# The norms of the latent vectors: squares, sums and roots made within the input projections, not beside the first neighbourhood heads

## The chip, the cores and the metric

The kernel runs on one core of a Trainium2 chip. The engines have the profile's short names: PE is TensorE (matrix products; PEld its weight loads), DVE is VectorE, ACT is ScalarE, POOL is GpSimd and SP is SyncE, which here only issues DMA transfers. The metric is the device time of one execution in microseconds (us), and the median of several executions is the time of a kernel. A profiled execution gives the trace from which the rows below are taken; its span is the time from its first to its last instruction.

## The reference

Two consecutive layers of a diffusion backbone work on 512 latent tokens and 256 context tokens of 1024 features. Layer 0 has two groups of heads that share one input projection: eight latent-attention heads and eight neighbourhood heads. The part that the change touches is the norm of the low-rank vectors of the latent-attention heads. For each token the projection gives 256 features for the queries (`cq`) and 128 for keys and values (`ckv`); each of the two is divided by the root of its mean square and multiplied by a gain before it is projected up:

```python
def rms_norm(x, gain=None):
    y = x * rsqrt(mean(x * x, axis=-1) + EPS)
    return y * gain

q    = rms_norm(p[..., :256], q_norm) @ w_q_up       # 8 heads of 64 + 32
c_kv = rms_norm(p[..., 256:384], kv_norm)            # keys and values of 8 heads
k_rope = p[..., 384:416]                             # 32 rotated features
```

The neighbourhood heads (64 features each) attend in a two-dimensional grid of the latent tokens, with a bias that masks what lies outside a neighbourhood, and to the context. After the heads come the output projection and a gated feed-forward layer. Layer 1 has 16 windowed heads in place of both groups, again with a feed-forward layer, and a last norm ends the program.

## The kernel before

All tensors are held with features on the 128 partitions and the 768 tokens (512 latent, 256 context) along the free dimension. A product in 32-bit precision is made of three products of halves: a high part and a low part of each operand, of which the two low parts' product is left out. Lines L324, L325 and L326 are these three products of the projections; L311 and L312 make the two halves of a weight, and L348 and L349 (`split`) those of an activation.

The projections of layer 0 are one generator, `projections`. It first makes the query and key pairs of neighbourhood heads 0 to 3, and then goes through the string `AFTER = "012k5678"`: "0", "1" and "2" are the three latent tiles `lat_raw[0..2]` of 128 features and 768 tokens (0 and 1 are `cq`, 2 is `ckv`), "k" is the rotated key, and "5" to "8" are raw queries and keys of heads 4 to 7. Between its steps, side work is taken in: the rows of the modulation (`mod_tile`, lines L241 to L262), which multiply weights by the conditioning vector `cond`, on DVE by L241, or on POOL by L258 and on ACT by L259. `cond` goes through Silu first (L163). At the end of the projections a part of the modulation is made by PE instead, from weights that arrive as `ph` and `pl` (L191).

Then `attend(na_jobs())` runs the neighbourhood heads. For each block of queries PE makes scores (L749, L750), DVE adds the bias and finds the maximum in one instruction (L546, `take`), ACT takes the exponential (L542, `exps`), PE turns the result (L483, `turned`), DVE or ACT copies it out of PSUM (L474, L475), and PE multiplies it with the values (L536, `weighted`). L458 to L466 (`finish_pair`) divide by the sums. The bias tiles come from memory into a pool of two buffers named `nb`, 384 KB each, so that a new one can be loaded only when an older one has been read. Beside the heads, side work advances step by step, a step ending at each `yield`: the norms of the latent vectors (`latent_norms`, which calls `gained`) come first, then what prepares the latent heads.

`gained` has the squares on POOL (L921, since `SQ = 1`), the sum of the two `cq` squares on DVE (L925), the sum over partitions on PE by products with a column of ones (L928), Sqrt on ACT (L931), the reciprocal on DVE (L932), a spread of the 12 columns over partitions (`spread`, L453, on PE, and a copy on ACT, L940), the gains on DVE (L943) and the split into halves (L348, L349). Sqrt, Exp and Silu are held in different tables of ACT, so a change from one to another shows as `ACT_TABLE_LOAD`.

The order of the instructions on each engine isn't written out by hand. A list scheduler, with a simulated timeline, orders the recorded program by readiness and priority; instructions of the side work have a priority lowered by `LOWER = 150`. Buffers come from pools by name (`b` 24, `p` 8, `ph` and `pl` 4 each, `nb` 2, and so on), and PSUM banks of general use come from a ring of seven entries, `"stsdtsd"`, whose letters are the tags `pss`, `pst` and `psd` in the trace. All loads with plain `dma` are issued by SP in one queue (L134).

Of the kernel before, what the change touches and what calls it, by code (L numbers as in the profile page):

```python
# [15 lines left out]
P = 128  # L16
# [84 lines left out]
def hybrid_kernel(ctx: ExitStack, tc, I, out):  # L101
# [230 lines left out]
    def PQ():  # L332
        return PS("d")
# [576 lines left out]

    def gained(groups):

        d, m = PQ(), NT // P
        n = m * len(groups)
        col = T("sm", [P, 6, 2]).rearrange("p a b -> p (a b)")[:, :n]
        for i, (tiles, _) in enumerate(groups):
            acc = None
            for t in tiles:
                s = B()
                if SQ:  # L920
                    G.tensor_tensor(s, t, t, op=ALU.mult)  # L921
                else:
                    S.activation(s, t, AF.Square)
                if acc is not None:
                    V.tensor_tensor(s, s, acc, op=ALU.add)  # L925
                acc = s
            for j in range(m):
                PE.matmul(d[:, i * m + j : i * m + j + 1], acc[:, j * P : (j + 1) * P], ones[:, :1], start=True, stop=True)  # L928
        for i, (tiles, _) in enumerate(groups):
            c = slice(i * m, i * m + m)  # L930
            S.activation(col[:, c], d[:, c], AF.Sqrt, bias=eps, scale=1.0 / (P * len(tiles)))  # L931
        V.reciprocal(col, col)  # L932
        yield
# [20 lines left out]
    def projections():  # L954

        for p in range(2):
            yield from project_shifted(I["w_in0"][p], put_q(sets[p][0]), scale=0.125)
            yield from project_shifted(I["w_in0"][p + 4], put_k(sets[p][1], KC[0]))
        for x in AFTER:
            if x in "012":  # L960
                lat_raw[int(x)] = B()
                yield from project_shifted(I["w_in0"][8 + int(x)], put(lat_raw[int(x)]))
            elif x == "k":
                kr.append(B())
                yield from project_shifted(I["w_kr"], put_rope(kr[0], rope0, SWAP8, 32, tag="p"), m=32)
            else:
                raws.append(B(tag="p"))
                i = int(x) - 5
                yield from project_shifted(I["w_in0"][(2, 6, 3, 7)[i]], put(raws[i]), scale=(0.125, None)[i % 2])

# [30 lines left out]
    def latent_norms():  # L1001
        groups = [(lat_raw[2:], 2), (lat_raw[:2], 0)]
# [906 lines left out]
```

## Time and profile before

| what | value |
|---|---|
| three executions | 1591.6, 1584.18 and 1589.64 us, median 1589.64 |
| the profiled execution: its time, its span | 1587.21 us, 1585.4 us |
| mean granted clock of PE | 0.995 |
| busy share of the span: PE, PEld, DVE, ACT, POOL | 97%, 87%, 75%, 51%, 17% |
| transfers over the whole span | 214.95 MB, mean 136 GB/s |
| the projections' end and the first neighbourhood heads | about 198 us of the span |
| start of the first roots of the latent norms (L931) | 220.79 us |

A row of a timeline gives the start, the duration, the engine, the line, the operation, output and inputs by their names, shapes, and how often it stands in a row; in brackets stands the idle time of the engine ahead of it and what ended that. A row of waits says what an engine waited for, with the total, the number and the longest. A row of the chain gives the start, the duration and the kind of work that set the end at that time.

### The profile page before, as it was taken

The numbers are of one execution on the slowest core, as the hardware profiler recorded it, in microseconds if no ns is written. First come the engines' busy times: TensorE is split into PE (matmuls) and PEld (weight loads), VectorE is DVE, ScalarE is ACT, GpSimd is POOL, SyncE is SP. The second block draws the span as 40 slices with busy tenths as digits, with TensorE's granted clock in tenths as the row PEclk, the third lists the DMA queues.
The fourth block names the chain that finished last, engine by engine and source line by source line (L and its number), as shares of the span: only waits on it lengthen the run. The fifth ranks groups of instructions, "written<-read, shape, count | busy, mean of one in ns | idle before, by whom it ended". The sixth has DMA issues, their size and how long they took to land.

```text
span 1585.4 us, 26844 instructions
## 1 busy us (share of the span) xinstructions
PE 1536.0 (97%) x10034; PEld 1372.4 (87%) x10034; DVE 1183.9 (75%) x2429; ACT 807.5 (51%) x1643; POOL 264.3 (17%) x290
## 2 busy tenths in 40 slices
PE   6998989999999999999999999999999999999998
PEld 4786877887898989899999999877889998898998
DVE  4495878668579789786867776868877778687686
ACT  5354487677366324242433345557756545354453
POOL 0151734330010110111111010393002000000000
PEclk9999999999999999999999999999999999999999
DMA  9445343101562564746647565131006133233332
GB/s 345 137 172 187 108 123 89 45 11 55 185 209 91 167 238 151 238 152 211 225 161 262 185 211 203 41 104 43 2 11 196 43 111 128 87 100 113 90 104 87
DMA packets 80852, 214.95 MB, mean 136 GB/s; under 512 B 10577, under 2 KB 18257, under 8 KB 80721
## 3 DMA queue, kind: packets, MB, share of 16 engines
q1 hardware_dynamic: 66640, 162.89, 32.0%
q0 software_dynamic: 11776, 47.19, 8.3%
q10 hardware_dynamic: 2304, 3.15, 0.5%
q8 instruction: 79, 1.29, 0.3%
q14 instruction: 53, 0.43, 0.1%
HBM read 186.97 MB, written 23.07 MB: 132 GB/s over the span
## 4 chain that ended last, share of the span: by engine, by line
PE 81%; DVE 9%; DMA 4%; issue 2%; ACT 2%; POOL 2%; SPq 0%; DVEq 0%; ACTq 0%; POOLq 0%
PE pso L536 5%; PE pss L1347 4%; PE pss L324 4%; PE pss L325 4%; PE pss L1346 4%; PE pss L1345 4%; PE pss L326 4%; PE psd L1345 3%; PE psd L1347 3%; PE psd L1346 3%; PE psd L324 3%; PE psd L325 3%; PE psd L326 3%; PE pst L1347 3%; PE pst L1345 3%; PE pst L1346 3%
## 5 line engine op out<-in xcount | busy, mean ns | idle before, releaser
L311 ACT CAST wh<-wr 128x512 fp32r<-128x512 f32 (+2 forms) x142 | 108.3, 777 | 197.0 <-PE pss L325 35.7
L312 DVE TENSOR_TENSOR wl<-wr,wh 128x1024 fp32r<-128x1024 f32 (+2 forms) x139 | 127.5, 924 | 78.5 <-ACT wh L311 77.9
L542 ACT ACTIVATE p<-p,sm 128x512 f32<-128x512 f32 (+3 forms) x144 | 105.0, 730 | 27.1 <-DVE sm L546 24.9
L325 PE MATMUL psd<-b,wh 128*128 128x256 f32 (+4 forms) x257 | 88.1, 343 | 0.0
L1347 PE MATMUL pss<-b,wl 128*128 128x256 f32 (+1 forms) x258 | 80.0, 310 | 2.5 <-DVE wl L1333 2.5
L324 PE MATMUL psd<-b,wh 128*128 128x512 f32 (+4 forms) x217 | 78.6, 362 | 2.1 <-ACT b L434 1.3
L1346 PE MATMUL pss<-b,wh 128*128 128x256 f32 (+1 forms) x258 | 79.8, 309 | 0.0
L1345 PE MATMUL pss<-b,wh 128*128 128x256 f32 (+1 forms) x258 | 79.4, 308 | 0.0
L536 PE MATMUL pso<-ph,b 128*64 128x256 f32 (+1 forms) x384 | 78.5, 363 | 0.3 <-DVE ph L474 0.2
L536 PE MATMUL pso<-pl,b 128*64 128x256 f32 (+1 forms) x384 | 77.9, 362 | 0.7 <-DVE pl L474 0.7
L324 PE MATMUL pss<-st,wh 128*128 128x256 f32 (+2 forms) x231 | 78.0, 338 | 0.5 <-ACT wh L311 0.5
L326 PE MATMUL pss<-st,wl 128*128 128x512 f32 (+2 forms) x231 | 77.8, 337 | 0.0
L326 PE MATMUL psd<-b,wl 128*128 128x512 f32 (+4 forms) x217 | 76.6, 354 | 0.0
L1346 PE MATMUL pst<-b,wh 128*128 128x384 f32 (+1 forms) x240 | 74.7, 311 | 0.0
L1345 PE MATMUL pst<-b,wh 128*128 128x384 f32 (+1 forms) x240 | 74.6, 311 | 0.0
L1347 PE MATMUL pst<-b,wl 128*128 128x384 f32 (+1 forms) x240 | 74.4, 311 | 0.0
L325 PE MATMUL pss<-b,wh 128*128 128x256 f32 (+4 forms) x227 | 74.0, 328 | 0.1
L1346 PE MATMUL psd<-b,wh 128*128 128x384 f32 (+1 forms) x222 | 69.8, 314 | 0.0
L1345 PE MATMUL psd<-b,wh 128*128 128x384 f32 (+1 forms) x222 | 69.7, 314 | 0.0
L1347 PE MATMUL psd<-b,wl 128*128 128x384 f32 (+1 forms) x222 | 69.6, 314 | 0.0
L1332 ACT CAST wh<-ph 128x512 fp32r<-128x512 f32 x80 | 46.3, 620 | 40.3 <-PE pst L1346 13.0
L1332 ACT CAST wh<-wr 128x1024 fp32r<-128x1024 f32 x40 | 42.0, 1051 | 41.8 <-PE pss L1346 16.1
(628 smaller groups left out, 5411.2 us busy)
## 6 DMA issues: line engine op xcount, KB each, us to landing
wr<-in_w_gu_dram SPq DMA_DIRECT2D x88, 512.0 KB, 4.1
wr<-in_w_out_dram SPq DMA_DIRECT2D x32, 512.0 KB, 3.6
wr<-in_w_dn_dram SPq DMA_DIRECT2D x64, 256.0 KB, 2.8
p<-home SPq DMA_DIRECT2D x40, 384.0 KB, 4.3
home<-p POOLq DMA_DIRECT2D x40, 384.0 KB, 5.1
nb<-in_mod_w_dram POOLq DMA_DIRECT2D x48, 256.0 KB, 3.8
rope<-in_mod_w_dram POOLq DMA_DIRECT2D x24, 512.0 KB, 4.0
wr<-in_w_in_dram SPq DMA_DIRECT2D x21, 512.0 KB, 4.1
```

What stands on the lines that cost most here:

```text
L311: S.copy(h, r)
L312: (G if eng else V).tensor_tensor(lo, r, f(h), op=ALU.subtract)
L324: PE.matmul(o, wh[:, k], mh[:, c], start=first and k == 0, stop=False)
L325: PE.matmul(o, wh[:, k], ml[:, c], start=False, stop=False)
L326: PE.matmul(o, wl[:, k], mh[:, c], start=False, stop=last and k == n - 1)
L536: ins = PE.matmul(o[64 * i : 64 * i + 64, c], v(kt), t, start=n == 0, stop=n == len(moving[i]) - 1)
L542: S.activation(p[:, c], p[:, c], AF.Exp, bias=nm, scale=-1.0, accum_out=dn)
L1332: S.copy(h, t)
L1345: PE.matmul(o, wh, xh, start=first and k == 0, stop=False, skip_group_check=not first)
L1346: PE.matmul(o, wh, xl, start=False, stop=False, skip_group_check=not first)
L1347: PE.matmul(o, wl, xh, start=False, stop=k == 3, skip_group_check=not first)
```

## The change

The squares and the sum of the two `cq` squares are made in `projections`, by `latent_squares`, as soon as the tiles "1" and "2" have been projected. `latent_roots` makes the products with ones, the roots and the reciprocals once projection "6" has been recorded, and puts the 12 columns into a tile of their own, `latent_cols`. `gained` begins with the spread. It has one `yield` less, so one step of side work less. The squares take `nb` buffers rather than `b` buffers. The two roots have a bank each from the ring (`PG`), where `gained` took one by `PQ`.

```diff
+    latent_cols = T("latent_cols", [P, 12])
+    def latent_squares(i):
+        acc = None
+        for t in latents()[i][0]:
+            s = T("nb", [P, NT])
+            G.tensor_tensor(s, t, t, op=ALU.mult)
+            if acc is not None:
+                V.tensor_tensor(s, s, acc, op=ALU.add)
+            acc = s
+        return acc
+    def latent_roots(accs):
+        m = NT // P
+        for i, acc in enumerate(accs):
+            d, col = PG(), latent_cols[:, i * m : i * m + m]
+            for j in range(m):
+                PE.matmul(d[:, j : j + 1], acc[:, j * P : (j + 1) * P], ones[:, :1], start=True, stop=True)
+            S.activation(col, d[:, :m], AF.Sqrt, bias=eps, scale=1.0 / (P * len(latents()[i][0])))
+            V.reciprocal(col, col)
+    def latents():
+        return [(lat_raw[2:], 2), (lat_raw[:2], 0)]
     def gained(groups):
-        d, m = PQ(), NT // P
-        n = m * len(groups)
-        col = T("sm", [P, 6, 2]).rearrange("p a b -> p (a b)")[:, :n]
-        for i, (tiles, _) in enumerate(groups):
-            acc = None
-            for t in tiles:
-                s = B()
-                if SQ:
-                    G.tensor_tensor(s, t, t, op=ALU.mult)
-                else:
-                    S.activation(s, t, AF.Square)
-                if acc is not None:
-                    V.tensor_tensor(s, s, acc, op=ALU.add)
-                acc = s
-            for j in range(m):
-                PE.matmul(d[:, i * m + j : i * m + j + 1], acc[:, j * P : (j + 1) * P], ones[:, :1], start=True, stop=True)
-        for i, (tiles, _) in enumerate(groups):
-            c = slice(i * m, i * m + m)
-            S.activation(col[:, c], d[:, c], AF.Sqrt, bias=eps, scale=1.0 / (P * len(tiles)))
-        V.reciprocal(col, col)
-        yield
+        col, m = latent_cols, NT // P
...
                 lat_raw[int(x)] = B()
                 yield from project_shifted(I["w_in0"][8 + int(x)], put(lat_raw[int(x)]))
+                if x in "12":
+                    accs.insert(0, latent_squares(int(x == "1")))
...
                 yield from project_shifted(I["w_in0"][(2, 6, 3, 7)[i]], put(raws[i]), scale=(0.125, None)[i % 2])
+                if x == "6":
+                    latent_roots(accs)
```

Three places show how the order of the instructions moves. The numbers behind names are buffer numbers, which differ between the two programs by the tiles added.

On PE, behind projection "6" and ahead of the next product with the context columns (258 wide), the changed program has (`ones` is the column of ones, `pst`, `pss` and `psd` are banks of the ring):

```order
L325 MATMUL pss_1693<-b_150,wh_1644 128x512
L326 MATMUL pss_1693<-b_149,wl_1645 128x512
L930 MATMUL pst_1736<-ones_92,nb_1460 128x1 x6
L930 MATMUL pss_1745<-ones_92,nb_1313 128x1 x6
L324 MATMUL psd_1761<-b_135,wh_1757 128x258
```

The same products stood between the turns (L483) and scores (L749) of the first neighbourhood heads before:

```order
L483 MATMUL psd_2151<-ident_r_88,wr_2103 128x128
L928 MATMUL psd_2182<-ones_92,b_2184 128x1 x5
L749 MATMUL pss_2158<-st_714,st_711 128x256
L750 MATMUL pss_2158<-st_715,st_711 128x256
L483 MATMUL psd_2151<-ident_r_88,p_2120 128x128
```

So 12 one-column products (two records each in the trace) went from the heads into the projections; in the heads the spread of the columns (L453) now stands where the first five of them stood.

On DVE, in the first neighbourhood heads, the program before has the reciprocal of the roots (L932) and the first gain (L943) at these places among the maxima (L546), behind the division's reciprocal (L458):

```order
L458 RECIPROCAL sm_2327<-sm_1949 128x12
L932 RECIPROCAL sm_2183<-sm_2183 128x12
L546 ISA wr_2305,sm_2125<-pss_2300,nb_2130 128x512
L546 ISA sm_2125 128x1
L546 ISA p_2324,sm_2125<-pss_2317,nb_2130 128x512
L546 ISA sm_2125 128x1
L474 COPY ph_2274<-pst_2269 128x512
L546 ISA p_2350,sm_2125<-pss_2343,nb_2127 128x512
L546 ISA sm_2125 128x1
L546 ISA p_2370,sm_2125<-pss_2367,nb_2127 128x512
L546 ISA sm_2125 128x1
L943 SCALAR_TENSOR_TENSOR b_1310<-b_1310,mla_gain_742,b_2217 128x768
```

and now:

```order
L949 SCALAR_TENSOR_TENSOR b_1316<-b_1316,mla_gain_743,b_2208 128x768
L546 ISA wr_2315,sm_2151<-pss_2310,nb_2156 128x512
L546 ISA sm_2151 128x1
L546 ISA p_2342,sm_2151<-pss_2335,nb_2156 128x512
L546 ISA sm_2151 128x1
L474 COPY ph_2286<-pst_2281 128x512
L546 ISA p_2352,sm_2151<-pss_2345,nb_2153 128x512
L546 ISA sm_2151 128x1
L349 TENSOR_TENSOR b_2221<-b_1316,b_2220 128x768
L546 ISA p_2372,sm_2151<-pss_2369,nb_2153 128x512
L546 ISA sm_2151 128x1
L949 SCALAR_TENSOR_TENSOR b_1112<-b_1112,mla_gain_743,b_2235 128x768
```

The first gain (L949, which was L943) now stands where the reciprocal stood, four maxima earlier than before, and its split L349 follows it by three maxima; the other two gains stand four maxima earlier too. The sum (L925, now L920) is no longer among them.

On SP, the loads that go out before the conditioning vector were

```order
L134 DMA ph_999<-in_mod_w_dram 128x512
L134 DMA pl_1003<-in_mod_w_dram 128x512
L134 DMA nb_1952<-in_nb_dram 128x768
L134 DMA cond_67<-in_cond_dram 128x1024 x2
L134 DMA wr_1012<-in_w_in_dram 128x1024
```

and at the end of the projections the changed program has

```order
L134 DMA ph_1916<-in_mod_wp_dram 128x512
L134 DMA nb_1977<-in_nb_dram 128x768
L134 DMA pl_1920<-in_mod_wp_dram 128x512
L134 DMA nb_1978<-in_nb_dram 128x768
L134 DMA ph_1944<-in_mod_wp_dram 128x512
```

The two bias loads that head 0 reads first went out early, one of them right ahead of `cond`; now both stand among the last weights of the modulation on PE, ahead of one `pl` and one `ph`.

On POOL the two squares of `cq` (L918) stand ahead of the products L258 that begin at 150.91 us in the trace of before, and the square of `ckv` three L258 later; all three stood behind the projections. The order of PE in the heads that follow, in the feed-forward of layer 0 and in layer 1's window stage differs in places, without an instruction more or less.

More of the change, by code (lines that the diff above doesn't have):

```diff
@@ L1001, in latent_norms @@
     def latent_norms():
[L1002 removed]
+        groups = latents()
         yield from gained(groups)
```

1 line of the change is left out of this document (added).

## The prediction

> **What bounds the kernel now.** I read the page's busy shares first, then a table of stages (stretches of the span in us; its columns are the length, the busy time and instruction count of TensorE, its weight loads, VectorE, ScalarE and GpSimd, the granted clock, the DMA share and GB/s), then inside the one stage that the change empties the waits and the chain.
>
> ```profile
> span 1585.4 us, 26844 instructions
> PE 1536.0 (97%) x10034; PEld 1372.4 (87%) x10034; DVE 1183.9 (75%) x2429; ACT 807.5 (51%) x1643; POOL 264.3 (17%) x290
> 70.00:85.00 15.00, 14.10 (x72) 10.91 (x71) 9.57 (x26) 10.23 (x19) 0.61 (x1) 1.00 0.93 333
> 120.00:150.00 30.00, 25.29 (x162) 18.65 (x163) 11.88 (x23) 13.47 (x28) 0.00 (x0) 0.94 0.55 192
> 150.00:198.00 48.00, 48.00 (x301) 37.77 (x293) 43.83 (x69) 22.88 (x55) 34.96 (x26) 1.00 0.42 122
> 198.00:250.00 52.00, 46.16 (x350) 36.92 (x350) 40.89 (x101) 44.18 (x104) 18.64 (x13) 1.00 0.41 115
> 250.00:350.00 100.00, 100.00 (x752) 82.19 (x751) 69.60 (x200) 72.28 (x169) 31.22 (x24) 1.00 0.16 47
> ```
>
> TensorE is busy 97% of the span, so time can only be won where it idles. The last 48 us of the projections (150 to 198) leave it none, nor do the 100 us after 250. Between them, in the first neighbourhood heads (198 to 250), it idles 52.00 - 46.16 = 5.84 us. This is the stage from which the squares, sums and roots of the norms are taken, and 150 to 198 is where the TensorE part of them is put. What TensorE waits for in the first heads, and the middle of the chain there:
>
> ```profile
> PE pss L749 <- DVE sm L546: 4.3, 5, 1.3
> 215.62 0.87 DVE b L925
> 219.90 3.08 DMA nb<-in_nb_dram
> 224.46 4.30 DMA nb<-in_nb_dram
> 228.89 0.69 DVE wr L546
> 230.55 0.87 DVE b L349
> 231.76 1.86 DVE b L943 x2
> ```
>
> 4.3 of the 5.84 us are waits of a score product for VectorE's bias-and-maximum (L546, which adds the neighbourhood bias `nb` to the scores). VectorE's own chain alternates: a bias tile can be loaded only when L546 has finished with one of its two buffers, so load, L546, load, L546. Rows of the norms sit in that chain: the sum L925 (0.87), a split L349 (0.87) and two gains L943 (1.86).
>
> **The change part by part.** The sum below is made against the profiled execution's own 1587.21 us (span 1585.4); the median of the three runs is 1589.64, so a forecast for the median is the sum plus 2.4.
>
> *A, the one-column products.* 24 records of TensorE leave the first heads and stand after projection "6", inside the stretch without idle time:
>
> ```profile
> 216.05 1.18 PE L928 MATMUL psd<-ones,b 128*128 128x1 f32 x10
> 217.09 0.37 PE L749 MATMUL pss<-st,st 128*128 128x256 f32 x1
> 218.42 0.95 PE L928 MATMUL psd<-ones,b 128*128 128x1 f32 x8
> 219.23 0.31 PE L483 MATMUL pst<-ident_r,p 128*128 128x128 f32 x1
> 219.70 0.73 PE L928 MATMUL psd<-ones,b 128*128 128x1 f32 x6
> 220.29 0.36 PE L749 MATMUL pss<-st,st 128*128 128x256 f32 x1
> ```
>
> From each group's start to the next instruction's: 217.09 - 216.05 = 1.04, 219.23 - 218.42 = 0.81, 220.29 - 219.70 = 0.59, in all 2.44. Nothing hides it at the new place: **+2.4**. Its bounds are 0 (a bubble swallows it) and 2.9 (the busy times 1.18, 0.95 and 0.73 added, without overlap).
>
> *B, the first heads.* TensorE's 2.44 us leave a stage in which it isn't the bound, which by itself gains nothing unless VectorE's chain becomes shorter. That chain loses L925 outright: 0.87. L349 and the two L943 (0.87 + 1.86 = 2.73) still have to be done, but no longer wait for the roots, and the new order puts the first gain ahead of the bias work and the split between two L546. They then fall into VectorE's waits for `nb` (2.8 us in this stage by the first row below, some of it taken by L925's removal); I let 2.2 of the 2.73 be hidden. The roots (L931, with its table load and the load back to Exp) and the reciprocal L932 cost more on paper than they are worth:
>
> ```profile
> DVE wr L546 <- DMA nb<-in_nb_dram: 2.8, 3, 2.1
> 220.79 1.28 ACT L931 ACT_TABLE_LOAD   x1
> 222.08 0.42 ACT L931 ACTIVATE sm<-psd,eps 128x6 f32<-128x6 f32 x2
> 222.52 1.28 ACT L542 ACT_TABLE_LOAD   x1
> 223.85 0.72 ACT L542 ACTIVATE wr<-wr,sm 128x512 f32<-128x512 f32 x1
> 222.54 0.23 DVE L932 RECIPROCAL sm<-sm 128x12 f32<-128x12 f32 x1 [1.81 <-ACT sm L931]
> 223.12 0.69 DVE L546 CUSTOM_DVE_ANT_0 wr<-pss,nb 128x512 f32<-128x512 f32 x1 [0.35 <-DMA nb<-in_nb_dram]
> ```
>
> The 3 us of ScalarE from 220.79 to 223.85 run beside the load that is on the chain from 219.90 to 222.98: VectorE, once done with the reciprocal at 222.77, waits 0.35 more for `nb`, and the exponential at 223.85 needs the maximum that L546 gives at 223.8. So removing them is worth about nothing while that load stays. Sum of B: -0.87 - 2.2 = **-3.1**. Bounds: 0 (the bias loads keep the stage's length) and -8.3 (all the idle 5.84 goes, and the 2.44 of products with it).
>
> One of the three table loads between the projections and these heads goes too (the roots now come between the projections' Silu and the heads' Exp, and the load back to Exp takes the place of the one that stood there): 1.28 us of ScalarE, behind which the next instruction started at once (222.52 + 1.28 = 223.80, then 223.85). [...]
>
> *C, two bias loads leave an early stretch.* Since the squares take the two `nb` buffers, the first two bias tiles are no longer loaded there but among the last modulation weights.
>
> ```profile
> 80.85 1.28 ACT L163 ACT_TABLE_LOAD   x1
> 74.25 0.37 SPq L134 DMA_DIRECT2D nb<-in_nb_dram  x1
> 74.72 1.11 SPq L134 DMA_DIRECT2D cond<-in_cond_dram  x2
> 185.82 0.33 SPq L134 DMA_DIRECT2D pl<-in_mod_wp_dram  x1
> ```
>
> At 70 to 85 the transfers are saturated (share 0.93, 333 GB/s), and 384 KB at that rate are 1.18 us that `cond` no longer waits. The first Silu of `cond`, whose table load is the 80.85 row, can start that much earlier; I take half, since ScalarE and VectorE need not be free at once: **-0.5**, bounds 0 and -1.2. At the other end the loads now stand on SP's queue ahead of one `pl` and one `ph` of modulation weights, and can't start before the one-column products have read the squares; the products that read those two come at 192.07 (its second repeat) and 196.05, and the last matmul ahead of the one-column products is the first row:
>
> ```profile
> 186.03 0.39 PE L326 MATMUL pss<-b,wl 128*128 128x512 f32 x1
> 192.07 0.41 PE L191 MATMUL pss<-pl,cond_col 128*32 128x256 f32 x2
> 196.05 0.41 PE L191 MATMUL pss<-ph,cond_col 128*32 128x256 f32 x2
> ```
>
> In the new order the one-column products follow the matmul of 186.03, whose end is at 186.4, so they end at about 188.8. The `pl` load then goes out near 189 rather than 185.82 and lands, behind 1.2 us of `nb` and in the 3.08 us that a larger load took in the chain, near 193.3; its use is at 192.3 + 2.4 = 194.7. That holds by 1.4 us: 0 in the sum, and up to 2 us lost if the landing takes longer.
>
> *D, squares, sum and roots at the new place.* GpSimd's three squares are 4.92 us, VectorE's sum 0.95, ScalarE's load and roots 1.28 + 2 x 0.26.
>
> ```profile
> 197.84 4.92 POOL L921 TENSOR_TENSOR b<-b 128x768 f32<-128x768 f32 x3
> 150.91 1.71 POOL L258 TENSOR_TENSOR ph<-ph,cond 128x512 f32<-128x512 f32 x1 [33.55 <-PE pss L191]
> 163.83 1.64 POOL L445 TENSOR_TENSOR p<-p,rope 32x512 f32<-32x512 f32 x1 [5.12 <-DVE p L443]
> 157.32 0.15 DVE L245 SCALAR_TENSOR_TENSOR mod<-mod,modb 128x1 f32<-128x1 f32 x1
> 153.11 1.24 DVE L245 SCALAR_TENSOR_TENSOR mod<-mod,modb 128x1 f32<-128x1 f32 x1
> ```
>
> Two squares come before GpSimd's work at 150.91, ahead of which it idles 33.55 us; the third comes into the 5.12 us before 163.83. VectorE has 30 - 11.88 = 18 us free in 120 to 150, ScalarE 25 in 150 to 198. All hidden: **0**, and at most 1.6 (the third square, which falls where VectorE is busy; R3 has the rest). The last two rows speak against me: the same one-column operation of VectorE takes 0.15 us alone and 1.24 beside a GpSimd product. [...]
>
> *E, what is shifted along.* Two more PSUM banks are taken from the ring of seven tags, so that each later user of the ring has another bank, and some instructions of layer 1's window stage change places:
>
> ```profile
> 1050.00:1075.00 25.00, 21.39 (x113) 16.83 (x113) 16.98 (x45) 12.79 (x25) 24.29 (x17) 0.93 0.52 168
> ```
>
> The idle time of TensorE there, 3.6 us, bounds it on both sides; I take **0**, as nothing says which way.
>
> Sum: 2.4 - 3.1 - 0.5 + 0 + 0 = -1.2, so 1586.0 for an execution like the profiled one, and 1588.4 for the median; I say **1588**. Put otherwise, TensorE's work stays the same and only its idle time in the first heads shrinks a little.
>
> **The rivals.**
>
> *R1, the products are paid and nothing comes back.* The bias loads (3.08 and 4.30 us in the chain) set the length of the first heads whatever VectorE does in between. For it: VectorE waits for `nb` in three places even now. Against it: L349 and both L943 stand on the chain when no load is on its way. Time: 1589.64 + 2.4, up to +4 with the modulation load of C late, so about **1592**, which is on the slower side by sign.
>
> *R2, the first heads lose all idle time.* With nothing of the norms between, TensorE runs full from the projections on. For it: 4.3 of the 5.84 us wait for L546 alone. Against it: `nb` loads remain. 1589.64 + 2.44 - 8.28 - 0.5 is about **1583**.
>
> [...]
>
> *R4, the shifted banks or layer 1's order decide.* Up to 3.6 us either way: **1585 to 1592**.
>
> *R5, the change does not do what it says.* The order of GpSimd and TensorE shows squares and products at the new place, so this has next to no chance.
>
> **How the numbers follow.** Forecast 0.52, R1 0.20, R2 0.13, R3 0.08, R4 0.07. The range runs from 1580 (R2 and the low bound of E together) to 1596 (R1 with 4 us of D and E, and short of R3): it leaves out about 2 in 10. Half a per cent is 7.9 us, about what a measurement of this kernel can tell from no change, so the bounds are 1581.7 and 1597.6. The forecast, R1 and R4 lie within, R2 mostly (0.08 of its 0.13 is past 1581.7 once run-to-run spread is added), R3 half. That gives faster 0.09, slower 0.07, same 0.84.
>
> **What would show it.** A: 24 one-column records near 187 to 190 and TensorE still without idle time in 150 to 198, which ends 2 to 3 us later than now. B: the stage that follows shorter by 4 to 6 us (2.44 of products and the 3.1), TensorE's idle time there between 1 and 5, no L925 or roots in its chain; if that idle time stays near 5.8 it is R1, if it is under 1, R2. C: the first Silu of `cond` starts before 80.85. D: GpSimd's squares before 150.91, no VectorE operation stretched beside them. I am wrong if the time moves by over 8 us, and my working is wrong if the moved L349 and L943 still stand on the chain.

## The result

The changed kernel takes 1594.45 us (median of 19 executions, 1587.66 to 1599.1) where the kernel before takes 1587.15 (19 executions taken beside it): a ratio of 1.0046 with a 95% interval of 1.0033 to 1.0058. It is slower by some 7 us. The ratio is just inside the half per cent that was set as no change (its interval reaches beyond), and the sign of the forecast (1.2 us faster) is wrong. Two executions of over 4600 us, one of e5 and the only one of e16, are left out of all numbers below.

The page of the changed kernel's profiled execution (1594.98 us):

```profile
span 1593.2 us, 26863 instructions
PE 1537.7 (97%) x10034; PEld 1375.0 (86%) x10034; DVE 1186.6 (74%) x2430; ACT 806.6 (51%) x1642; POOL 265.7 (17%) x290
```

TensorE is busy 1.7 us longer and idle 6.1 us longer (55.5 for 49.4). To see where, both traces were cut at the same instructions of TensorE. In the rows below, the idle time of TensorE is the length less its busy time. Stretches of the kernel before (columns as in the table of stages above; the stages are the products' new place, the first heads, the first feed-forward layer's start, its weight loads, layer 1's window heads):

```profile
176.00:195.00 19.00, 19.00 (x117) 15.86 (x116) 17.88 (x32) 9.58 (x25) 13.63 (x13) 1.00 0.48 134
195.00:300.00 105.00, 99.16 (x754) 79.59 (x753) 78.90 (x200) 81.71 (x191) 42.08 (x33) 1.00 0.35 99
480.00:560.00 80.00, 79.19 (x463) 72.59 (x462) 66.68 (x128) 36.35 (x69) 5.39 (x10) 1.00 0.42 137
560.00:600.00 40.00, 38.06 (x210) 35.87 (x209) 34.63 (x69) 13.55 (x23) 7.02 (x13) 0.96 0.62 206
1040.00:1140.00 100.00, 95.91 (x686) 77.48 (x685) 75.51 (x248) 71.42 (x163) 44.22 (x32) 0.98 0.16 52
```

and the same work in the changed kernel:

```profile
172.20:193.80 21.60, 21.60 (x141) 18.48 (x140) 18.06 (x34) 11.16 (x28) 14.31 (x14) 1.00 0.56 163
193.80:296.30 102.50, 97.43 (x730) 78.04 (x730) 79.25 (x198) 77.93 (x187) 36.83 (x29) 0.98 0.35 100
478.60:560.10 81.50, 79.12 (x463) 72.70 (x462) 65.56 (x125) 36.65 (x69) 5.39 (x10) 1.00 0.40 131
560.10:603.10 43.00, 38.04 (x209) 35.58 (x209) 35.47 (x71) 13.30 (x23) 7.01 (x13) 0.96 0.60 197
1044.00:1146.60 102.60, 97.49 (x686) 78.93 (x685) 73.92 (x250) 72.29 (x163) 43.45 (x32) 0.97 0.16 50
```

The products cost 2.6 us where they now stand, and the first heads are 2.5 us shorter. So far the two cancel. In this pair of traces the loss comes where no line was changed: +1.5, +3.0 and +2.6 us in the last three rows, and 2.3 more between 300 and 480 us of before. The second traces, below, show which of these come again.

The second thing to see is the clock. The mean granted clock of the 19 executions is 0.9915; that of the kernel before, over the 133 executions that stand beside all runs below, is 0.9943. Over all executions of all kernels, each kernel with its own level, the time falls by 1.29 us for each 0.001 of clock. By this fit, which is an estimate, the 0.0028 of clock go with 3.6 us of the loss, and about 3 us are left at equal clock. In the trace the clock is either full or half, and half for windows of 3.41 us (or twice that) on a fixed grid. Ahead of the program's end the trace of before has three (at 143, 587 and 1072 us, which lie 130 and 142 such windows apart) and a second trace of it two (23 and 583); the changed kernel has seven (22, 118, 234, 387, 589, and two in a row at 1063), and seven in its second trace too.

What makes such a window is shown by the first new one. Three windows of the changed kernel:

```profile
114.30:117.70 3.40, 0.36 (x2) 0.34 (x3) 3.18 (x9) 2.92 (x8) 0.61 (x1) 1.00 0.56 134
117.70:121.10 3.40, 3.40 (x10) 2.62 (x9) 3.24 (x7) 3.33 (x8) 0.00 (x0) 0.51 0.45 121
121.10:124.50 3.40, 3.40 (x16) 2.79 (x15) 2.73 (x6) 2.09 (x5) 0.00 (x0) 0.99 0.61 211
```

TensorE works 0.36 of 3.40 us, and in the window behind it the clock is 0.51. The wait in the changed kernel, first row, and the two waits of before that it took the place of:

```profile
117.34 0.47 PE L324 MATMUL psd<-b,wh 128*128 128x512 f32 x1 [3.36 <-DVE st L720]
```

```profile
122.72 0.39 PE L324 MATMUL pst<-b,wh 128*128 128x258 f32 x1 [1.62 <-DVE st L720]
133.96 0.36 PE L324 MATMUL pst<-b,wh 128*128 128x258 f32 x1 [1.28 <-DVE st L720]
```

Behind the idle time of 1.62 us, and behind that of 1.28, no window of half clock begins; behind the 3.36 us in one place one does. Such a window costs about 1.7 us of TensorE's work (an estimate: half of its 3.41 us). How busy TensorE was in the windows ahead of such ones is counted over 19 traces in the last section.

### The profile page after: what moved, and what is told of

It reads as the page before. It is cut to its first block, busy times and chain, and to the rows that moved or that the text cites. A ratio compares the mean times of both kernels' runs of the same rounds, so it can differ in the third digit from the quotient of the medians.

```text
span 1593.2 us, 26863 instructions
## 1 busy us (share of the span) xinstructions
PE 1537.7 (97%) x10034; PEld 1375.0 (86%) x10034; DVE 1186.6 (74%) x2430; ACT 806.6 (51%) x1642; POOL 265.7 (17%) x290
## 3 DMA queue, kind: packets, MB, share of 16 engines
q8 instruction: 79, 1.29, 0.3%
## 4 chain that ended last, share of the span: by engine, by line
PE 69%; issue 13%; DVE 9%; DMA 4%; POOL 3%; ACT 2%; SPq 0%; POOLq 0%; DVEq 0%; ACTq 0%
PE pso L536 5%; PE pss L1358 3%; PE pss L324 3%; PE pss L1356 3%; PE pss L1357 3%; PE pss L325 3%; PE pss L326 3%; PE psd L324 3%; PE psd L325 3%; PE psd L326 3%; PE psd L1358 2%; PE pst L483 2%; PE psd L1356 2%; PE psd L1357 2%; PE pst L324 2%
## 5 line engine op out<-in xcount | busy, mean ns | idle before, releaser
L1358 PE MATMUL pss<-b,wl 128*128 128x384 f32 (+1 forms) x324 | 102.2, 315 | 5.8 <-DVE wl L1344 5.8
L1356 PE MATMUL pss<-b,wh 128*128 128x384 f32 (+1 forms) x324 | 101.8, 314 | 0.0
L1357 PE MATMUL pss<-b,wh 128*128 128x384 f32 (+1 forms) x324 | 101.6, 314 | 0.0
L324 PE MATMUL psd<-b,wh 128*128 128x512 f32 (+4 forms) x212 | 79.2, 374 | 6.9 <-ACT b L434 3.5
L325 PE MATMUL psd<-b,wh 128*128 128x512 f32 (+4 forms) x236 | 84.1, 356 | 0.0
L324 PE MATMUL pss<-st,wh 128*128 128x256 f32 (+2 forms) x230 | 76.8, 334 | 0.6 <-ACT st L1343 0.6
L326 PE MATMUL pss<-st,wl 128*128 128x256 f32 (+2 forms) x230 | 76.6, 333 | 0.0
L1356 PE MATMUL psd<-b,wh 128*128 128x384 f32 (+1 forms) x240 | 74.5, 311 | 0.0
L1357 PE MATMUL psd<-b,wh 128*128 128x384 f32 (+1 forms) x240 | 74.3, 310 | 0.0
L1358 PE MATMUL psd<-b,wl 128*128 128x384 f32 (+1 forms) x240 | 74.1, 310 | 0.0
L1358 PEld LDWEIGHTS pss<-b,wl 128*128 128x128 f32 x324 | 61.4, 189 | 7.0 <-DVE wl L1344 7.0
L483 PE MATMUL pst<-ident_r,p 128*128 128x128 f32 x346 | 60.6, 281 | 1.7 <-DVE ph L474 0.8
L749 PE MATMUL pss<-st,st 128*128 128x256 f32 (+3 forms) x194 | 58.9, 328 | 3.1 <-DVE sm L546 2.8
L1356 PEld LDWEIGHTS pss<-b,wh 128*128 128x128 f32 x324 | 61.5, 190 | 0.4 <-ACT p L1406 0.2
```

Of the source, the lines that this page charges most:

```text
L324: PE.matmul(o, wh[:, k], mh[:, c], start=first and k == 0, stop=False)
L325: PE.matmul(o, wh[:, k], ml[:, c], start=False, stop=False)
L326: PE.matmul(o, wl[:, k], mh[:, c], start=False, stop=last and k == n - 1)
L483: ins = PE.transpose(o[:, i * P : (i + 1) * P], b, ident)
L749: PE.matmul(o, x, ks[0][:, keys], start=True, stop=False)
L1356: PE.matmul(o, wh, xh, start=first and k == 0, stop=False, skip_group_check=not first)
```

## The experiments

Theory 1: the other PSUM banks cost it. Theory 2: the norms' new place does. Theory 3: the other order of layer 1's window heads. Theory 4, formed after the first four runs: each part loses at its own places. Theory 5, formed after the first eight: what a part costs is less the sum of TensorE's idle time than the windows of half clock that idle time in one piece brings. All ratios are to the kernel before on the same chip.

**Giving the ring back (e1).**

```diff
                 if x == "6":
                     latent_roots(accs)
+                    ring[0] -= 2
```

> The changed kernel with one line more: the two turns that the roots take of the ring of PSUM banks are given back behind them, so every later user of the ring has the bank tags that it had before. In the traces the changed kernel is 3.7 us ahead of the kernel before at 370 us and 7.7 us behind at the end. Theory 1 (the shifted banks cost what is lost after 370 us): the time is 2 to 4 us under the kernel before, ratio 0.997 to 0.999, and lag stays near -3.7 through 1050 us. Theory 2 (the norms' new place, or where its time falls against the windows of the TensorE clock, costs it): the ratio stays at 1.003 to 1.006 as in the changed kernel. Theory 3 (the other order of layer 1's window stage costs it; this kernel still has most of that order): about 1.000, with the loss between 1050 and 1130 us alone.

Measured 1.0038 (1.0020 to 1.0055). The banks are not all of it; by this run, with 1.0046 for the changed kernel, they are the smaller part.

**The banks alone (e2).** The kernel before, with

```diff
+                if x == "6":
+                    ring[0] += 2
```

> The kernel before with one line more: the ring of PSUM banks is turned on by two at the place where the roots would stand (behind projection 6). Nothing of the norms moves; later users of the ring have the bank tags of the changed kernel. Theory 1 (shifted banks): 8 to 11 us over the kernel before, ratio 1.005 to 1.007, with steps of the lag near 390, 505, 587 and 1060 us. Theory 2 (the norms' new place): ratio 0.999 to 1.001. Theory 3 (layer 1's order): 2 to 4 us, ratio 1.0015 to 1.0025, all of it between 1050 and 1130 us.

1.0040 (1.0020 to 1.0059): the banks alone, with nothing of the norms moved, cost about as much as the whole change. So theory 2 does not hold alone either. In its trace the start of the feed-forward layer is 1.5 us longer than in before, and layer 1's window heads 1.1:

```profile
479.30:560.80 81.50, 79.13 (x463) 72.59 (x462) 65.95 (x126) 36.77 (x69) 5.39 (x10) 1.00 0.40 134
1043.80:1144.90 101.10, 96.04 (x687) 77.94 (x686) 73.86 (x250) 72.13 (x163) 44.19 (x32) 0.98 0.15 50
```

The costs of e1 and e2 (0.38 and 0.40%) don't add up to the change's 0.46%: in e2 the banks cost 0.40%, in e1 giving them back takes 0.08% away.

**One step of side work less (e3).** The kernel before without the first `yield` of `gained`.

> The kernel before without the first yield of the norms: one step of side work less, everything else at its old place and with its old bank tags. Its order differs from before in the first neighbourhood heads and in layer 1's window stage (the same 519 rows of TensorE as in the run that gives the ring back). Theory 3 (layer 1's order costs it): 2 to 4 us over, from 1050 us on. Theories 1 and 2: within 1.5 us of the kernel before, ratio 0.999 to 1.001.

1.0041 (1.0023 to 1.0060), over what theories 1 and 2 expected, and not at theory 3's place. Its loss is in the first heads: 112.1 us where before has 105.0, 9.6 of them idle, with two windows of half clock. One step of side work less made that stage 7.1 us longer.

**Another turn of the ring (e4).** As e2 with `ring[0] += 5`, which leaves the order nearly alone.

> The kernel before with the ring of PSUM banks turned on by five in place of two at that place. The order of the instructions of all engines hardly differs from before (some 30 rows of TensorE, 4 of VectorE), but every later user of the ring has another bank. Theory 1, if the bank tags by themselves cost: several us over, like the turn by two. Theory 1b, if the tags cost by the order that the scheduler makes of them: within 1.5 us of the kernel before, ratio 0.999 to 1.001. Theory 2 expects the same as 1b.

0.9993 (0.9977 to 1.0008). Turned by five the ring costs nothing that this run shows, turned by two it gave 1.0040. Whether that comes of the banks themselves or of the order that the scheduler makes of them was not shown.

**Layer 1's order alone (e5) and other banks in layer 1 alone (e6).** The kernel before, ahead of layer 1's heads, with 2 in e5 and 5 in e6:

```diff
     H = new
+    ring[0] += 2
```

> The kernel before with the ring of PSUM banks turned on by two only ahead of layer 1's heads (after the first feed-forward layer). All orders are those of before up to about 1040 us; behind it layer 1's window stage has the order that the changed kernel has there, and nothing else moves. All four slow kernels so far (the changed one, the ring given back, the ring turned by two, no yield) share such an order there, and the two that aren't slow (before, the ring turned by five) don't. Theory 3 (layer 1's order alone): ratio 1.003 to 1.005 (5 to 8 us), with the loss between 1040 and 1140 us and behind it. Theory 4 (each slow kernel loses at its own places: first heads, 480 to 600 us, layer 1 by about 1 us): 0 to 2 us over, ratio 1.000 to 1.0015.

> As the run before, but turned on by five at that late place: other banks for all ring users of layer 1, the order of VectorE and ScalarE that of before and TensorE's moved in some 18 rows. Theory 3 (the order): ratio 0.999 to 1.001. If the banks by themselves cost, 2 us or more over. For theory 4 it is a second look at an unchanged program up to 1040 us: between 560 and 600 us TensorE should idle about 2 us, as in before and the ring turned by five (1.9 and 2.4), where the four slow kernels had 3.8 to 5.0.

0.9997 (0.9980 to 1.0015) and 0.9995 (0.9982 to 1.0008). Theory 3 falls: the order that all four slow kernels share costs nothing on its own that these runs can tell from zero. Between 560 and 600 us e6, which is the kernel before up to 1040 us, has 3.8 us of idle time, so part of the +3.0 us there in the first trace is chance.

**Squares in the pool `b` (e7).** As e1 with `s = B()` for the squares.

> The changed kernel with the ring's turns given back and the squares in buffers of the general pool b in place of the two bias buffers, so that the first bias tiles are loaded early again, ahead of the conditioning vector. Part C of the prediction said that the early loads cost 0.5 us (0 to 1.2) and the late ones nothing. By that it is 0 to 1.2 us over the kernel with the ring given back, ratio to before 1.003 to 1.005. If the late bias loads hold the first heads, it is 2 us or more under that kernel, ratio 1.001 to 1.003.

1.0065 (1.0040 to 1.0090), a miss: the order changed once more, the products stand in two groups some 11 us apart, and TensorE waits 2.8 us between them (L324 for ACT's L436). It says nothing on the bias loads.

**A second trace of before (e8).**

> The kernel before itself, for a second trace of it. If the stall between 560 and 600 us is a property of the kernel, TensorE idles about 2 us there again; if it is a matter of the single execution, it may be 4 us as in the slow kernels.

Between 560 and 600 us it has 3.6 us of idle time, where the first has 1.9; the two traces of the changed kernel have 5.0 and 2.4. So the loss seen there changes from execution to execution. In the other stages of the table the second trace has 19.0, 104.7, 80.0 and 98.4 us, close to the first but for layer 1's heads, where the first has a window of half clock and is 1.6 us longer. In the projections from 50 to 176 us it is 3.3 us shorter (122.7 for 126.0): it has no window at 143 us and 1.7 us less idle time.

**Late bias loads alone (e9).** The kernel before, behind projections "1" and "2":

```diff
+                if x in "12":
+                    for t in lat_raw[int(x) // 2 * 2 : int(x) + 1]:
+                        G.tensor_copy(T("nb", [P, NT])[:, :1], t[:, :1])
```

> Part C alone: the kernel before, with three one-element copies into the two bias buffers behind the latent projections 0 to 2, so that the first two bias tiles are loaded late, as in the changed kernel. TensorE's order in the projections stays that of before; VectorE makes the first modulation sum (L241) ahead of the first L709, as in the changed kernel. In the traces of the changed kernel and of the one with the ring given back TensorE waits 3.3 us in one piece near 115 us, where before has two waits of 1.6 and 1.3 at 121 and 133 us, and a window of half clock follows (117.8 and 120.2). Theory 5 (idle time in one piece costs a half-clock window, 1.7 us, though its sum is the same): one wait of over 3 us near 115 and a half-clock window behind it; 1.5 to 2.5 us over before, ratio 1.001 to 1.0015. The prediction's part C: 0 to 1.2 us under before. If it is 4 us or more over, C is most of the whole loss.

The wait in one piece comes, and the window at 118.1 us with it; the time is 0.9999 (0.9979 to 1.0018). The waits ahead of 130 us of this kernel:

```profile
PE psd L324 <- DVE st L720: 3.3, 1, 3.3
```

So part C shows no effect on the time, within about 3 us on either side. That the clock (0.9934, beside 0.9943) took back a gain of 1 us is possible, but these runs don't separate it.

**Products and first heads alone (e10).** As e1 with the squares in the pool `p`, so that the bias tiles are loaded early.

```diff
-            s = T("nb", [P, NT])
+            s = T("p", [P, NT])
```

> Parts A and B alone: the changed kernel with the ring's two turns given back and the squares in buffers of the pool p, so that the bias tiles are loaded early as before and VectorE's order near 115 us is that of before. By the prediction's parts A and B it is 0.7 us under before, ratio 0.999 to 1.000. Theory 5 (the ring given back still lost by the wait in one piece near 115 us): no wait over 2 us before 195 us, no half-clock window near 118, and 2 to 4 us under the kernel with the ring given back: ratio 1.0005 to 1.002. If it stays at 1.004, the products in the projections and the new order of the first heads cost all of it.

1.0020 (1.0001 to 1.0039). No window stands near 118 us, as theory 5 has it, but one stands where nothing waits. Three windows of this kernel, the products' first:

```profile
172.60:176.00 3.40, 3.40 (x29) 3.27 (x28) 3.33 (x7) 0.77 (x3) 1.32 (x2) 1.00 0.25 77
176.00:179.40 3.40, 3.40 (x17) 3.40 (x17) 3.40 (x5) 0.57 (x2) 2.74 (x2) 0.50 0.44 154
179.40:182.80 3.40, 3.40 (x20) 2.95 (x19) 3.37 (x9) 3.06 (x6) 2.71 (x3) 1.00 0.28 83
```

and what the first of them holds, from TensorE's timeline (in records, two for each product):

```profile
173.21 1.40 PE L930 MATMUL pst<-ones,p 128*128 128x1 f32 x12
174.47 1.48 PE L930 MATMUL pss<-ones,p 128*128 128x1 f32 x12
175.81 0.39 PE L324 MATMUL pst<-b,wh 128*128 128x258 f32 x1
```

TensorE counts as busy for 3.40 of 3.40 us, most of it with products of one column, and the next window has half clock: the move costs 23.2 - 19.0 = 4.2 us there. e1 has the same (23.2 us, window at 178.2). The changed kernel's first trace has no such window. Where the products fall against the clock's grid differs; this is their busy time alone (L930) in the grid's windows, first in the changed kernel, then in e10:

```profile
172.36:175.77 3.41, 1.83 (x18) 2.02 (x18) 1.00 0.27 77
175.77:179.18 3.41, 0.91 (x9) 0.82 (x8) 1.00 0.55 153
```

```profile
172.60:176.01 3.41, 2.73 (x24) 2.83 (x24) 1.00 0.25 77
```

In the first, the edge of a window cuts the piece in two, so that neither window is filled. The first heads of e10 are 105.7 us long with 7.4 us idle: the changed kernel's gain there is absent.

**The products after "k" (e11).** As e10 with `latent_roots` behind the rotated key's projection.

> As the run before, but products and roots follow the projection of the rotated key rather than projection 6, some 25 us earlier, next to the stretch (120 to 150 us) where TensorE has 3 to 5 us of idle time. If that idle time takes the one-column products in, stage 176 to 195 us is 19.0 us long again and the time is 1 to 2.5 us under the run before. If they wait for the squares there, a new wait stands near 150 us and the time is the same or longer.

1.0030 (1.0012 to 1.0047). The idle time before 150 us takes nothing in: the stretch ahead of the 19.0 us stage is 126.9 us long, 4.2 more than in the second trace of before (122.7; the first, with its own window there, has 126.0), with the window at 160.7. The first heads are not shorter here either (105.1 us).

**The products split (e12) and doubled (e13).** As e10; in e12 three products behind each of "5" to "8", each group with its own bank (the lines below show the call alone); in e13 each product twice.

```diff
-                if x == "6":
-                    latent_roots(accs)
+                if x in "5678":
+                    latent_roots(accs[i < 2], int(i < 2), 3 * (i % 2))
```

> As the kernel with the squares in p (parts A and B alone, 1.002), but the twelve one-column products are split: three each behind projections 5, 6, 7 and 8, each with a bank of its own that is given back to the ring. In that kernel, in the one with the ring given back and in the one with the products after k, a half-clock window follows the clock window that the products fill, though TensorE is busy all through it (1.00): 176.0, 178.2 and 160.7 us. Theory 5b (products of one column count as idle time for the clock; twelve in one piece fill a window): no half-clock window between 150 and 195 us, the stages from 110 to 195 us shorter by 1.7 us, ratio 1.000 to 1.002. If the window there came from something else, it stays, and the ratio stays at 1.002 or more.

> As the kernel with the squares in p, but each one-column product is made twice, one piece of about 4.9 us in place of 2.4. Theory 5b: the piece fills a whole clock window wherever it falls, so a half-clock window follows in every execution, two in some; stage 176 to 195 us is 19.0 + 4.9 + 1.7 = 25.6 us or longer; 2.5 to 5 us over the kernel with the squares in p, ratio 1.0035 to 1.005. If products of one column cost just their own time, 2.4 us over it, with no window more.

Split: no window of half clock between 60 and 195 us, so that part came true. The whole is 1.0016 (1.0002 to 1.0030), not to be told from e10, as the trace has three windows in the first heads instead. The first of these, at 198.8 us, stands behind the last group of three, in a window that also has 0.5 us of idle time. Doubled: the stage is 25.9 us long with one window, as expected (19.0 + 4.9 + 1.7), but the whole is 1.0022 (1.0006 to 1.0038), not the 1.0035 expected. The first heads are 102.0 us in that trace against 105.7 of e10, so part of the delay came back there; why, and whether it does in all executions, was not shown.

**Other banks from 200 to 1040 us (e14).** As e2, with `ring[0] += 5` ahead of layer 1's heads.

> The kernel before with the ring of banks turned by two behind projection 6, and by five more ahead of layer 1's heads, so that the banks are other ones from 200 to 1040 us only. The ring turned by two for good gave 1.0040, and turned by two from 1040 us on 0.9997. In the traces with other banks TensorE waits 1.4 and 0.8 us for an eviction from the bank at 497 and 510 us where before has 0.8 once. If the part before 1040 us holds the cost of the banks: 4 to 7 us over before, ratio 1.0025 to 1.0045. If it is only these waits of 1.5 us: 1 to 2 us, ratio 1.0005 to 1.0015, and the rest of the cost comes from both parts together.

1.0019 (1.0003 to 1.0036), between the two cases. With e5's 0.9997 that makes 1.0016 of e2's 1.0040; the intervals touch, and a part that needs both stays open.

**The mildest form (e15).** As e12 with the squares in `nb` again.

> The changed kernel with what the runs so far showed as avoidable taken out: the ring's turns given back, and the products split in four behind projections 5 to 8; the squares stay in the bias buffers, so the bias loads are late. By the parts measured: products 2.4, first heads -2.6 with a half-clock window now and then (1.3), late bias loads 0, no window at the products: about 1 us over before, ratio 0.9995 to 1.0015. If the change is worth something in any form, it is under 0.9985.

1.0025 (1.0010 to 1.0041), slower than expected. Its mean is 3.8 us over that of before beside it, and by the fit the clock (0.9922 beside 0.9948) goes with 3.3 of them. Its trace has the wait of 3.3 us with its window, and none at the products. No form of the change was faster than the kernel before.

**Second traces (e16, e17, e18).** The changed kernel twice and e2's kernel once more.

> The changed kernel itself, for a second trace. What belongs to the kernel comes again: one wait of 3.3 us near 115 us with a half-clock window, the waits of 1.4 and 0.8 us near 497 and 510 us, one of 3.5 us near 1060 us with a half-clock window. What belonged to the one execution (the window at 387 us, idle time of 5.0 us between 560 and 600 us) may be gone. After the products at 175 us a half-clock window may stand, as in three of the kernels that have them in one piece.

> The changed kernel itself once more for a second trace (the execution before this one was disturbed, 4944 us). What belongs to the kernel comes again: one wait of 3.3 us near 115 us with a half-clock window behind it, the waits of 1.4 and 0.8 us near 497 and 510 us, a wait of 3.5 us near 1060 us with a half-clock window. The window at 387 us may be gone, and one may stand behind the one-column products at 175 us.

> The ring of banks turned by two, for a second trace. What belongs to the other banks comes again: 1.5 us more idle time between 480 and 560 us, the wait of 3.5 us near 1060 us with a half-clock window; the first heads and the projections are those of before.

e16 took 4944 us and tells nothing. e17 (1595.21 us) has the wait of 3.3 us and its window again, and behind the products two windows, so that the stage is 24.7 us long:

```profile
174.30:177.70 3.40, 3.40 (x27) 3.18 (x26) 3.37 (x6) 0.67 (x3) 1.41 (x2) 1.00 0.24 77
177.70:181.10 3.40, 3.40 (x18) 3.40 (x18) 3.36 (x7) 0.67 (x3) 2.64 (x2) 0.51 0.53 156
181.10:184.50 3.40, 3.40 (x15) 3.23 (x15) 3.37 (x8) 2.98 (x6) 2.71 (x3) 0.50 0.36 97
```

The window at 387 us is gone, and one stands at 478 instead: these belong to single executions. What the banks do came again in both kernels. The waits of TensorE at the feed-forward layer's start, in the changed kernel and then in before (its second trace):

```profile
PE pss L1356 <- ACT p L1395: 1.4, 1, 1.4
PE pss L1356 <- ACT p L1402: 0.8, 1, 0.8
```

```profile
PE psd L1345 <- ACT p L1384: 0.8, 1, 0.8
```

and at the start of layer 1's window heads, likewise (before here by the trace of the prediction):

```profile
PE psd L324 <- ACT b L434: 3.5, 1, 3.5
```

```profile
PE pss L749 <- DVE sm L546: 1.6, 2, 1.2
PE psd L324 <- ACT b L434: 1.3, 1, 1.3
```

At the first place TensorE waits for copies that ScalarE makes out of banks (L1395, L1402) for 1.4 + 0.8 us, where before has 0.8 in all (80.0 us become 81.3 to 81.5 in all traces with these banks, e14's too). In layer 1, waits of 1.3 us at most become one of 3.5 (3.6 in e18), with half clock behind it in all four traces; before has a window there in one of its two.

Measured alone, the parts are 0.40% for the banks, -0.01% for the late loads and 0.20% for products and first heads, in all 0.59%; together they are 0.46% (0.33 to 0.58). With intervals of about 0.2% for each part that is no contradiction, but it is no proof of this division either: by e1, giving the banks back takes only 0.08 of the 0.46% away.

## Why the prediction was wrong

**What bounds the kernel**: right. TensorE is the bound, and the 48 us of projections that had no idle time before have none in the changed kernel:

```profile
150.00:198.00 48.00, 48.00 (x300) 38.61 (x297) 41.79 (x68) 23.18 (x57) 33.69 (x25) 1.00 0.43 127
```

**A, the products at 2.4 us: mis-sized.** As time on TensorE they are 2.6 (21.6 - 19.0). What was left out is the clock behind them: the stage is 21.6, 24.7, 23.2 and 23.2 us in the two traces of the changed kernel, e1 and e10, so +4.2 on average. Before, the same products stood in groups of 10, 8 and 6 records among wide ones; no window of half clock stands near them in the two traces of before. With the products in one piece the window came where they filled most of a window of the grid, and with the split it was gone from this stage in both traces (e12, e15). So by these traces the piece is its cause; that the split saves time was not shown (1.0016 and 1.0020).

**B, the first heads at -3.1 beside the 2.4 that leave: mostly wrong.** The stage was to be 5.5 us shorter. It is 2.5 and 2.4 shorter in the two traces. Idle time there fell from 5.8 to 5.1 us (4.8 in the second trace), not by 3.1: about the 0.87 us of L925, which is gone. The step that failed is that L349 and two gains would fall into the waits for `nb`. They have moved, but stand on the chain as before. Rows of the changed kernel's chain:

```profile
201.78 2.99 DMA nb<-in_nb_dram
217.82 3.33 DMA nb<-in_nb_dram
223.68 0.87 DVE b L349
225.16 0.65 DVE b L949
226.01 1.01 DVE b L949
```

The last three are 2.53 us, between maxima. Bias loads run beside them (issued at 222.50 and 225.19 us), but VectorE doesn't wait for these: it reaches the next maximum on a new tile at 226.94 us, and finds the load of 222.50 landed at 225.76. Only the first gain, at 219.12, stands in a wait for `nb`, and it did so before (227.54). In size this is the rival R1. Its mechanism holds in part only: two bias loads, 6.3 us, are on this chain, where the chain of before had four, 13.5 us, and the stage kept most of its idle time all the same. A window of half clock comes on top in both traces of the changed kernel (at 234 and 239 us).

**C, -0.5: not contradicted, not shown** (e9: 0.9999, 0.9979 to 1.0018). The first Silu's table load did start earlier than at 80.85:

```profile
77.78 1.28 ACT L163 ACT_TABLE_LOAD   x1
```

But with the late loads one wait of 3.3 us came in place of two, which e9 shows alone, and which the working did not see. That it comes of L241 standing ahead of L709 on VectorE is likely and was not tested. The modulation weight behind the bias loads was in time: TensorE has no wait there.

**D, 0: right.** Two of the squares run before GpSimd's products there (147.01 us in this trace), and TensorE does not wait between 150 and 195 us. R3 (chance 0.08), that GpSimd's squares hold up VectorE until TensorE stalls, was the author's estimate, and no run shows such a stall. Beside the third square one sum of VectorE, L261, took 1.27 us, where the next took 0.16 with GpSimd idle, and TensorE waited for neither.

```profile
133.36 1.47 POOL L918 TENSOR_TENSOR nb<-b 128x768 f32<-128x768 f32 x1 [18.44 <-ACT sm L809]
135.90 1.93 POOL L918 TENSOR_TENSOR nb<-b 128x768 f32<-128x768 f32 x1 [1.08 <-ACT b L436]
152.77 1.91 POOL L918 TENSOR_TENSOR nb<-b 128x768 f32<-128x768 f32 x1
153.43 1.27 DVE L261 TENSOR_TENSOR mod<-part,part 128x1 f32<-128x1 f32 x1
156.72 0.16 DVE L261 TENSOR_TENSOR mod<-part,part 128x1 f32<-128x1 f32 x1 [0.78 <-ACT pl L259]
```

**E, 0 with 3.6 us on both sides: the term that was put at nothing without a reason.** It was bounded by the idle time of one stage of layer 1, though the order was seen to differ in the feed-forward layer too. The banks alone cost 0.2 to 0.6%, some 6 us (e2); within the changed kernel, by e1, their share may be far smaller. R4 named the mechanism with a chance of 0.07 and at most 3.6 us. The working took each stage's idle time as the most that a shift can add or take, as if it could not grow and as if its shape had no price.

**The clock** stood in no term. By the fit it goes with 3.6 of the 6.6 us by which the means differ (1593.7 and 1587.1); the windows looked at above stand behind waits and behind the products, so for these it is no further cause, but the price of their shape. The changed kernel's time lies inside the range of 1580 to 1596, as it was made wide for the cases on both sides, which is luck; the value and the sign were wrong. The forecast of 1588 also rested on a median of three executions, 1589.64, where 19 give 1587.15.

What stays open: how the loss of the changed kernel divides between the banks and the rest (e1 and e2 give different answers), how much of the banks' cost is in which place (e5 and e14 come to 0.16% of e2's 0.40%), why the first heads lack their gain in e10 and e11, and why the mildest form still has a clock 0.002 lower than before.

## What to carry to other kernels

Where the tensor engine is the bound, don't only add up its idle time: list its pieces against the clock's windows of 3.41 us, since 3.3 us in one place brought a window of half clock, about 1.7 us, that 1.6 and 1.3 us in two places did not. Price very narrow products in one piece with the clock behind them: here the stage became 4.2 us longer on average, where the products took 2.6 as time on TensorE. Among wide ones no window stood near them in two traces, and in groups of three one followed in one case of eight. And two turns of a shared ring of banks reached far behind their place here (near 1060 us one wait of 3.5 us where before had 1.3 at most, and 1.0040 in all by the turn alone): measure such a turn by itself before the change is judged, as its cost is not the idle time that was there.

## What the hardware showed

In 19 traces (60 to 1570 us of each, cut into the clock's own windows of 3.41 us) a window in which TensorE was busy under half the time was followed by half clock in 40 of 43 cases, between 0.5 and 0.6 in 14 of 37, and from 0.6 on in 16 of 8327 (of these, in the first traces of before and of the changed kernel: 6 of 6, 2 of 3 and 1 of 876). Of these 16, six have a busy share of 1.00, and all six hold one-column products.

In six traces (the changed kernel's two, e1, e10, e11 and e13) these products stand in one piece, of 24 records or, in e13, 48. Where they were busy for 2.27 to 3.41 us of a window (e17, e1, e10, e11, e13), half clock followed, five times of five; where the grid gave them 1.83 us of a window or less (the first trace of the changed kernel, and the first of e13's two windows), it did not. So in these traces half clock followed such products much as it followed idle time. The sixth window is the second of e17's two, which holds only their end; why half clock went on there stays open. Of eight groups of three products (e12, e15) one had half clock behind it, in the window with 0.5 us of idle time.
